# Convolution by single 128-channel blocks, a written order that reaches one group further, and another place for some tiles, in a two-layer decoder kernel

## The chip, the core and the metric

The kernel runs on one core of a Trainium2 chip. The metric is the device time of one execution in microseconds (us), as the median of three runs.

## What is computed

Two layers; in each, four parts add to the residual stream `h` (256 rows of 1024, float32):

```python
h = h + 0.5 * swiglu(rms_norm(h, ffn1_norm), w_gate_up, w_down)            # D_FF = 2816
u = rms_norm(h, mix_norm); q, k, v, ca, cg = split(u @ w_in)               # 512, 128, 128, 512, 512
attn = sliding_window_attention(rope(q), rope(k), v, sinks)                # 8 heads, 2 kv heads, window 128
conv = silu(layer_norm(depthwise_causal_conv31(ca * sigmoid(cg)) + b))     # 512 channels, 31 taps
h = h + concat(rms_norm(attn), rms_norm(conv)) @ w_out
h = h + 0.5 * swiglu(rms_norm(h, ffn2_norm), w_gate_up2, w_down2)
h = h + sigmoid(h @ w_gate) * rms_norm(p @ w_ple)
# after the layers: out = rms_norm(h, final_norm)
```

## The kernel before

The 256 rows are two blocks `t` of 128 rows. Nearly every product is made of three matmuls in the type fp32r: a float32 weight is split into a rounded part `hi` (a cast on ScalarE, ACT) and a rest `lo` (a subtraction on VectorE, DVE, or on GpSimd, POOL), the left operand likewise, and hi·hi, lo·hi and hi·lo are added in PSUM (`triple`, L262). Weights come by DMA in pieces of 512 KB into tiles tagged `raw` (4 buffers); `hi` and `lo` have 10 buffers each. A class `Unit` (L168) does this, either all at once (`load`, L174) or as named steps (`piece`, L208: `dma`, `hi`, `lo`, halves of 512 columns).

In every matmul of the projections and of the gate and up products the weights move through the array (512 columns, or 256) and a transposed block of the normalised input (`xh` or `xl`, 128 x 128) is stationary. In the down products the stationary tile is a slice of `hT_hi` or `hT_lo`, the transposed hidden block, and in the convolution's half of the output product it is a slice of `c_hi` or `c_lo`. These four come from the ring of tiles tagged `wr` (`wr`, L152; 4 buffers).

**The feed-forward stages** (`ffn_stage`, L425) run over 11 groups `j` of 256 hidden columns: load, gate and up for both row blocks (24 matmuls each), a transpose of the hidden block (`tr`, L449), the down products of the group before (24 matmuls). The compiler's scheduler orders all of this.

**The mixer stage** (`mixer_stage`, L652, `mixer`, L683) is different: the instructions of all five engines follow an order written out by hand, `PLAN` (L68), a list of step names. It begins inside the last two groups of the feed-forward stage before it (`dnb..`, `dnc..`, `fepi..`) and ends with the first group of the one behind it (`gu0`, `gu1`, with its loads `uf0`). Each engine does its own steps in that order. In it:

- the convolution's input comes in two column groups of 256 channels (`c0`, `c1`); `sig`, `u`, `ut`, `uT` gate and transpose it. Of the 31 taps the first 10 (8 in the second group) are done as a product on ACT (`pp`) that POOL adds up (`ya`), the rest as multiply-adds on DVE (`tap`, L756), each on two channel blocks of 128 in turn;
- `kv`, `q` with their rotary steps, then per head group the scores `s`, a fused mask-add and maximum on DVE (`ttr`, L875), `exp` on ACT, transposes `ptr`, copies `pT` (half on DVE, half on ACT), the products `pv`, the normalisation `o`;
- `ple`: float32 products for the layer's last part; `wa`, `wc`: the attention's and the convolution's half of the output product, then `xtr`, `xg`, `xh`, `xl` make the input of the next feed-forward stage.

`POOL_TAPS`, `QP`, `WCP` (L41 to L45) say which work POOL has: of `q` and `wc` it makes all `lo` halves. The softmax tiles `sm` (`sink`, L857) take two buffers of the `wr` ring for the first block and an own tag `pr` for the second. They are 2064 bytes per partition long, so the ring's buffers are 2080 bytes apart, the length rounded up to 32 bytes:

```python
            sm = wk.tile([P, n, NKV, P * (b + 1) + 1], F32, tag="wr" if b == 0 else "pr", name="sm",
                         bufs=NWR if b == 0 else 1)
```

The tiles' places follow from the order of the pools. In the built program the first weight tile stands at byte 44,960 of each partition, 32 beyond a multiple of 128; `xh` and `xl` also stand 32 beyond one, and the four `wr` buffers stand 32, 64, 96 and 0 beyond one.

Of the kernel before, what the change touches and what calls it, by code (L numbers as in the profile page):

```python
# [29 lines left out]
G = 4  # L30
# [10 lines left out]
POOL_TAPS = (10, 8)  # L41
C0P = ()
C1P = ()
QP = tuple(range(8))
WCP = tuple(range(4))  # L45
# [19 lines left out]
NPP = 2  # L65
# [27 lines left out]
rden1 pT100 yntr0 hwa01 ptr101 silu00 wa00.1 pT101 silu01 silu02 silu03 ptr111 hwa00 csq0 ptr110 pv100 ca0 pT111
chi0 fr0 pT110 clo0 yntr1 frs0 pv101 silu10 frr0 silu11 pv110 silu12 silu13 pv111 csq1 ca1 wc01.0 o1 chi1 clo1 osq1
wc01.1 rA1 fr1 hwc01 otr1 frs1 xtr01 frr1 oa1 wc00.0 xg01 wa11.0 wc00.1 uf0.hi3.0 uf0.hi3.1 wa11.1 uf0.lo3.0 hwc00
uf0.lo3.1 stat0 wa10.0 hwa11 uf0.hi2.0 rr0 uf0.hi2.1 wa10.1 uf0.lo2.0 uf0.lo2.1 xtr00 hwa10 wc11.0 xg00 xh00 wc11.1
xl00 wc10.0 xh01 hwc11 xl01 wc10.1 gu0.0 hwc10 stat1 xtr10 xtr11 xg10 gu0.1 rr1 xg11 xh10 xl10 gu0.2 xh11 gu0.3 xl11
gu1.0 sg0 h10 gu1.1 gu1.2 gu1.3 sg1 h11
# [4 lines left out]
def hybrid_trunk_kernel(  # L103
# [193 lines left out]

    ident = cp.tile([P, P], F32, name="ident")
# [126 lines left out]
    def ffn_stage(l, wgu, wdn, gname, side, early):  # L425
        X, r = [None, None], [None, None]
        H1, HT, DN, GU, acc = {}, {}, {}, {}, []
# [56 lines left out]
        def steps(does):  # L484

            GU[0] = unit_pair(wgu, 0, FF, KD)
            GU[0].steps("uf0", does)
            DN[0] = unit_plain(wdn, 0, 2, 0, D)
# [61 lines left out]

        def rest(nxt):
            for _ in range(2):
                acc.append([abank() for _ in range(2)])
            for j in range(NFC):
                if j > 0:
                    load(j)
                    gu(j, 0, GU[j])
                    tr(j - 1)
                if (j, 1) not in H1:
                    gu(j, 1, GU[j])  # L560
                if j in side:
# [64 lines left out]
    uT = [cp.tile([P, 2, CW - 1 + 256], F32, name=f"uT{e}") for e in range(2)]  # L626
# [3 lines left out]
    def mixer_consts():  # L630
# [8 lines left out]
        for e in range(2):  # L639
            GP.memset(uT[e][:, :, 0:CW - 1], 0.0)  # L640
# [11 lines left out]
    def mixer_stage(l, PT, EMB):  # L652
# [4 lines left out]
        c0 = unit_pair(w, 768, 1280, KD)  # L657
# [11 lines left out]
        def rest(nxt):  # L669
            c0.load(subs=2)  # L670
# [3 lines left out]
            mixer(l, w, X, r, r8, rotr, c0, PT, EMB, does)  # L674
# [8 lines left out]
    def mixer(l, w, X, r, r8, rotr, c0, PT, EMB, does):  # L683
# [3 lines left out]
        def halves(x, n=4):  # L687
# [19 lines left out]
        for name, label in (("c0", "c0t"), ("c1", "c1t"), ("kv", "kv"), ("q", "q")):  # L707
            for t in range(2):
                for s in range(KD // U[name].ku):
                    put(f"{label}{t}.{s}", part, name, t, s)  # L710

        def sig(e, t):
            tmp["sg", e, t] = wk.tile([P, FC], F32, tag="sg", name="sig", bufs=NSG)
            S.activation(tmp["sg", e, t], B[f"c{e}", t][:, FC:2 * FC], AF.Sigmoid, scale=r[t])

        def u(e, t):
            tmp["u", e, t] = wk.tile([P, FC], F32, tag="h1", name="u", bufs=NH1)
            V.scalar_tensor_tensor(out=tmp["u", e, t], in0=B[f"c{e}", t][:, 0:FC], scalar=r[t], in1=tmp["sg", e, t],
                                   op0=ALU.mult, op1=ALU.mult)

        def ut(e, t):
            if t == 0:
                tmp["ut", e] = tbank()
            for c in range(2):
# [3 lines left out]
        def to_uT(e):  # L728
            S.copy(uT[e][:, :, CW - 1:], halves(tmp["ut", e], 2))
# [508 lines left out]
```

## Time and profile before

| what | value |
|---|---|
| median of 3 runs | 1026.77 us (1026.62 to 1028.57) |
| the profiled execution's own time | 1029.06 us |
| its span, first to last instruction | 1027.2 us |
| TensorE (PE) busy | 998.3 us, 97% |
| DVE / ACT / POOL busy | 632.5 / 551.4 / 144.9 us |
| mean granted TensorE clock | 0.996 |

Times in the profile count from the first instruction. L12 is line 12 of the kernel. PE is the matmul, PEld the load of the stationary tile beside it. A matmul's recorded duration covers its way through a pipeline, so matmuls overlap; the pace is the distance of two starts. A matmul in plain float32 has two records, each of two passes.

### The profile page before, as it was taken

How to read it: one execution, taken by the hardware profiler on the slowest of the kernel's cores; microseconds unless marked ns; L12 is line 12 of the kernel's file. 1: busy time of each engine (PE TensorE's matmuls, PEld its weight loads, DVE VectorE, ACT ScalarE, POOL GpSimd, SP SyncE). 2: the span in 40 equal slices, each digit the busy share in tenths (PEclk: the TensorE clock that was granted, in tenths of full speed). 3: DMA queues.
4: the chain of work that ended last, by engine and by line, in shares of the span. 5: the costliest groups of instructions: out<-in, count | busy, mean ns of one | idle time of the engine just before them, and what ended most of it. 6: DMA issues, size and time to landing. Idle time of an engine off the chain costs nothing.

```text
span 1027.2 us, 13385 instructions
## 1 busy us (share of the span) xinstructions
PE 998.3 (97%) x4574; PEld 800.8 (78%) x4574; DVE 632.5 (62%) x1108; ACT 551.4 (54%) x1030; POOL 144.9 (14%) x195
## 2 busy tenths in 40 slices
PE   7999999999899999999999999999989999999996
PEld 5888888777577888888888888887857688888886
DVE  5864545679777554555775555547895955455553
ACT  6654444668754444445564445446885644444442
POOL 4300000067312000000000000001871300000001
PEclk9999999999999999999999999999999999999999
DMA  8865656444346565656556565644440666565621
GB/s 260 283 211 164 195 180 202 127 157 151 104 141 196 174 204 165 205 164 205 164 171 206 168 206 171 205 150 165 157 151 21 202 188 205 167 205 171 209 90 41
DMA packets 133172, 177.23 MB, mean 173 GB/s; under 512 B 8952, under 2 KB 109648, under 8 KB 133104
## 3 DMA queue, kind: packets, MB, share of 16 engines
q1 hardware_dynamic: 132016, 174.11, 53.1%
q0 software_dynamic: 1088, 2.27, 0.9%
q8 instruction: 36, 0.59, 0.2%
q14 instruction: 32, 0.26, 0.1%
HBM read 175.29 MB, written 1.05 MB: 172 GB/s over the span
## 4 chain that ended last, share of the span: by engine, by line
PE 89%; DVE 8%; DMA 1%; issue 1%; ACT 1%; SPq 0%; POOLq 0%; DVEq 0%; POOL 0%; ACTq 0%
PE bank L271 48%; PE abank L271 22%; PE bank L284 7%; PE bank L977 4%; DVE abank L756 3%; PE abank L525 2%; DVE lo L159 2%; PE tbank L453 2%; DMA raw<-in_ffn_w_gate_up_dram 1%; DVE xl L159 1%; DVE sm L875 1%; PE abank L907 1%; PE tbank L368 1%; PE tbank L396 0%; DVE xg L402 0%
## 5 line engine op out<-in xcount | busy, mean ns | idle before, releaser
L159 DVE TENSOR_TENSOR lo<-raw,hi 128x512 fp32r<-128x512 f32 (+1 forms) x507 | 378.5, 793 | 173.0 <-ACT hi L194 160.0
L194 ACT CAST hi<-raw 128x512 fp32r<-128x512 f32 (+1 forms) x464 | 303.4, 701 | 196.1 <-PE abank L271 118.2
L271 PE MATMUL bank<-hi,xh 128*128 128x512 f32 (+1 forms) x744 | 293.7, 395 | 1.4 <-ACT hi L194 1.2
L271 PE MATMUL bank<-hi,xl 128*128 128x512 f32 (+1 forms) x744 | 290.0, 390 | 1.0 <-DVE xl L159 1.0
L271 PE MATMUL bank<-lo,xh 128*128 128x512 f32 (+1 forms) x744 | 290.1, 390 | 0.3 <-POOL lo L159 0.2
L271 PEld LDWEIGHTS bank<-hi,xl 128*128 128x128 f32 x744 | 140.2, 188 | 31.0 <-DVE xl L159 2.2
L271 PEld LDWEIGHTS bank<-hi,xh 128*128 128x128 f32 x744 | 140.5, 189 | 29.7 <-ACT hi L194 1.6
L271 PEld LDWEIGHTS bank<-lo,xh 128*128 128x128 f32 x744 | 140.3, 189 | 29.5 <-POOL lo L159 1.3
L271 PE MATMUL abank<-hi,hT_hi 128*128 128x512 f32 x320 | 127.4, 398 | 0.0
L271 PE MATMUL abank<-lo,hT_hi 128*128 128x512 f32 x320 | 126.3, 395 | 0.0
L446 DVE SCALAR_TENSOR_TENSOR h<-bank,r,sg 128x256 f32<-128x256 f32 x84 | 40.5, 482 | 138.3 <-ACT sg L444 138.3
L271 PE MATMUL abank<-hi,hT_lo 128*128 128x512 f32 x320 | 125.5, 393 | 0.0
L444 ACT ACTIVATE sg<-bank,r 128x256 f32<-128x256 f32 x84 | 39.7, 473 | 159.5 <-PE bank L271 159.5
L348 POOL TENSOR_SCALAR ms_eps<-ms 128x1 f32<-128x1 f32 x24 | 6.6, 276 | 517.4 <-ACT scratch L355 208.4
L271 PEld LDWEIGHTS abank<-hi,hT_lo 128*128 128x128 f32 x320 | 60.2, 188 | 14.6
L271 PEld LDWEIGHTS abank<-hi,hT_hi 128*128 128x128 f32 x320 | 60.1, 188 | 13.6
L271 PEld LDWEIGHTS abank<-lo,hT_hi 128*128 128x128 f32 x320 | 60.2, 188 | 12.8
L756 DVE SCALAR_TENSOR_TENSOR abank<-uT,wconv,abank 128x256 f32<-128x256 f32 x168 | 69.2, 486 | 0.0
L284 PE MATMUL bank<-hi,xh 128*128 128x512 f32 (+1 forms) x160 | 62.0, 388 | 0.0
L284 PE MATMUL bank<-hi,xl 128*128 128x512 f32 (+1 forms) x160 | 59.3, 371 | 2.1 <-DVE xl L159 2.1
L284 PE MATMUL bank<-lo,xh 128*128 128x512 f32 (+1 forms) x160 | 59.0, 369 | 0.0
L227 ACT CAST hi<-raw 128x512 fp32r<-128x512 f32 x80 | 46.5, 615 | 21.2 <-PE bank L977 12.3
(183 smaller groups left out, 948.0 us busy)
## 6 DMA issues: line engine op xcount, KB each, us to landing
raw<-in_ffn_w_gate_up_dram SPq DMA_DIRECT2D x352, 256.0 KB, 4.0
raw<-in_ffn_w_down_dram SPq DMA_DIRECT2D x88, 512.0 KB, 5.4
raw<-in_w_in_dram SPq DMA_DIRECT2D x32, 256.0 KB, 3.8
raw<-in_w_out_dram SPq DMA_DIRECT2D x16, 512.0 KB, 4.9
raw<-in_w_ple_gate_dram SPq DMA_DIRECT2D x16, 512.0 KB, 4.2
raw<-in_w_in_dram SPq DMA_DIRECT2D x12, 512.0 KB, 4.6
raw<-in_w_ple_dram SPq DMA_DIRECT2D x4, 512.0 KB, 3.2
h<-in_x_dram SPq DMA_DIRECT2D x4, 256.0 KB, 4.5
```

The source lines that it names most:

```text
L159: return eng.tensor_tensor(out=lo, in0=src, in1=hi.bitcast(F32), op=ALU.subtract)
L194: S.copy(hi[:, sl, :], raw[:, sl, :])
L227: S.copy(half(sub[0], q), half(raw[0], q))
L271: T.matmul(dst, a, b, start=first and i == 0, stop=last and i == n - 1)
L284: T.matmul(dst, a, b, start=k == 0 and i == 0, stop=k == KD - 1 and i == 2)
L368: T.transpose(tb[:, i * P:(i + 1) * P], h[t][:, c * P:(c + 1) * P], ident)
L444: S.activation(s, b[:, 0:FC], AF.Silu, scale=r[t])
L446: V.scalar_tensor_tensor(out=o, in0=b[:, FC:2 * FC], scalar=r[t], in1=s, op0=ALU.mult, op1=ALU.mult)
L453: T.transpose(tb[:, k * 256 + t * P:k * 256 + (t + 1) * P], H1[j, t][:, k * P:(k + 1) * P], ident)
L525: T.matmul(acc[t][n], a, w_, start=False, stop=j == c and k == 1 and i == 2)
L756: V.scalar_tensor_tensor(out=acc, in0=src, scalar=ws, in1=acc, op0=ALU.mult, op1=ALU.add)
L977: T.matmul(B[name, t, n], a, b_, start=k == 0 and i == 0, stop=k == 3 and i == len(terms) - 1)
```

## The change

Four things change together.

1. **The convolution goes by blocks of 128 channels.** The group `c0` becomes `ca` and `cb` with 128 channels each (256 moving columns); `c1` becomes `cc`. `yp`, `pp`, `ya`, `tap` and `y` work on one block. 12, 12, 8 and 8 taps are POOL's, `pp` has 4 buffers.
2. **The order is new and longer**: 597 steps for 479. `kv` and `q` come before the third and fourth block. It takes in the loads `uf1` and the first 24 matmuls (`gux0`) of the second feed-forward group. The instructions of ACT and DVE that the groups `j` = 1 and 2 still trace are queued behind `sg1` and `h11` (`issue_after`: an order of issue on that engine, no wait).
3. **Work moves between engines**: the `lo` halves of `q` go from POOL to DVE, the copies `pT` all to ACT.
4. **Places**: the softmax tiles get tags of their own (`pr0`, `pr1`), their length rounded up to 128 bytes, so that the `wr` buffers are 2048 bytes apart; a tile of 96 bytes is put into the first pool, ahead of the weight and work pools. At the end `hf` and `o` take buffers of other tags.

```diff
-POOL_TAPS = (10, 8)
-QP = tuple(range(8))
+POOL_TAPS = (12, 12, 8, 8)
+QP = ()
+GROUPS = (("ca", (0,)), ("cb", (1,)), ("cc", (2, 3)))
-NPP = 2
+NPP = 4
...
+sigtab dnb11.0 ucb.dma0 ucb.dma1 ukv.dma0 ukv.dma1 dnb11.1 dnb00.0 ucb.hi0.0 dnb10.0 ucb.hi0.1 dnb10.1 ukv.hi0.0
...
+mxtr01 mxl00 uq.dma3 dnc10.1 mxg01 uq.hi1.0 mrr0 fepi10 uq.hi1.1 mxh01 fepi11 mxtr10 uq.hi2.0 mxl01 mxtr11 mrot0
+mxg10 uq.hi2.1 cat0.0 mxg11 mstat1 uq.lo0.1 cbt0.0 mxh10 uq.lo1.0 mrr1 ucc.dma0 uq.hi3.0 mxl10 uq.hi3.1 cbt0.1 mrot1
...
+uwc0.lo0.1 uwc1.hi0.0 uwc0.lo1.0 s00 uf0.dma0 sig20 ple00 ttr000 uwc1.hi0.1 u20 exptab uwc0.lo1.1 ttr001 ut20 ut21
+plesq00 uwc1.lo0.0 s01 uf0.dma1 s02 uT3 ttr010 uT2 ple10 tap3.8 yp3 uwc1.lo0.1 tap2.8 yp2 ttr011 tap2.9 pp3.1 ttr020
...
+pT111 tap2.30 pv101 uf0.lo1.0 silutab uf0.dma3 pv110 hwa00 uf0.lo1.1 pv111 y3 wa01.1 y2 uf1.dma0 o1 uf0.lo0.0 osq1
+otr1 uf0.lo0.1 rA1 ytr0 oa1 uf1.dma1 bn0 ytr1 wa10.0 bn1 lnr0 hwa01 lnr1 wa10.1 yn0 uf0.hi2.0 uf0.hi2.1 yn1 yntr0
...
+xl10 xtr11 gux0.0 xg11 gux0.1 xh11 xl11 gux0.2 gux0.3 gu0.2 sgx0 h1x0 gu1.0 gu0.3 gu1.1 sg0 h10 gu1.2 gu1.3 sg1 h11
...
+    cp.tile([P, 24], F32, name="pad")
     ident = cp.tile([P, P], F32, name="ident")
...
+        def one(j):
+            if j > 0 and (j, 0) not in H1:
+                load(j)
+                gu(j, 0, GU[j])
+            if j > 0:
+                tr(j - 1)
+            if (j, 1) not in H1:
+                gu(j, 1, GU[j])
...
             for j in range(NFC):
+                with ExitStack() as behind:
+                    for ins in last.values() if j == 1 or j == 2 else ():
+                        behind.enter_context(tc.issue_after(ins.ins))
+                    one(j)
...
-        c0 = unit_pair(w, 768, 1280, KD)
+        ca = unit_pair(w, 768, 1280, KD, cn=P)
...
-            c0.load(subs=2)
+            ca.load()
...
+        def pp(ch, k):
+            tmp["pp", ch, k] = wk.tile([P, 256], F32, tag="pp", name="pp", bufs=NPP)
+            S.activation(tmp["pp", ch, k], uT[ch][:, k:k + 256], AF.Copy, scale=wconv[l][:, ch:ch + 1, k])
+        def ya(ch, k):
+            GP.tensor_tensor(out=tmp["yp", ch], in0=tmp["yp", ch], in1=tmp["pp", ch, k], op=ALU.add)
...
         def sink(b, g0):
-            n = 2 if b == 0 else G
-            sm = wk.tile([P, n, NKV, P * (b + 1) + 1], F32, tag="wr" if b == 0 else "pr", name="sm",
-                         bufs=NWR if b == 0 else 1)
+            n, c = (2, P + 1) if b == 0 else (G, 2 * P + 1)
+            sm = wk.tile([P, -(-n * NKV * c // 32) * 32], F32, tag=f"pr{b}", name="sm", bufs=2 - b)
...
-            (V.tensor_copy if kv == 0 else S.copy)(tmp["pT", b, kc, kv], tmp["pt", b, kc, kv])
+            S.copy(tmp["pT", b, kc, kv], tmp["pt", b, kc, kv])
...
-                hf[t] = wk.tile([P, 512], F32, tag="pp", name="hf", bufs=NPP)
+                hf[t] = wf("hf")
-            o = wk.tile([P, 512], F32, tag="y", name="o", bufs=2)
+            o = wk.tile([P, 512], F32, tag="wr", name="o", bufs=NWR)
```

## Rows read from the trace of the kernel before

**Rows 1.** The page: busy time, share of the span, instructions.

```profile
PE 998.3 (97%) x4574; PEld 800.8 (78%) x4574; DVE 632.5 (62%) x1108; ACT 551.4 (54%) x1030; POOL 144.9 (14%) x195
```

**Rows 2.** Stretches of the span: length, each engine's busy time, clock, DMA.

```profile
22.50:190.40 167.90, 167.86 (x759) 137.66 (x760) 96.63 (x158) 82.82 (x139) 12.63 (x35) 1.00 0.64 200
...
190.40:316.40 126.00, 118.98 (x568) 88.97 (x567) 103.06 (x232) 88.92 (x204) 57.96 (x66) 1.00 0.42 138
...
692.40:820.00 127.60, 120.69 (x568) 89.77 (x567) 102.92 (x232) 88.77 (x203) 58.15 (x66) 0.99 0.42 137
...
204.90:243.00 38.10, 37.99 (x188) 30.83 (x187) 30.55 (x78) 27.75 (x65) 24.59 (x22) 1.00 0.47 165
243.00:268.20 25.20, 20.59 (x93) 13.08 (x92) 25.20 (x85) 20.51 (x57) 19.40 (x22) 1.00 0.45 148
...
770.00:785.00 15.00, 15.00 (x77) 10.09 (x75) 8.23 (x17) 10.19 (x29) 3.04 (x6) 0.89 0.11 35
```

**Rows 3.** The chain that ended last: start, length, engine, tile, line, count.

```profile
58.95 5.44 PE bank L271 x24
...
105.41 5.57 PE abank L271 x24
...
122.37 5.55 PE abank L271 x24
...
225.87 1.72 PE abank L271 x4
...
230.91 1.43 PE bank L284 x12
...
276.54 0.87 PE tbank L896 x8
277.42 0.84 PE abank L907 x8
...
282.33 2.84 PE bank L977 x12
```

**Rows 4.** The same chain, from 249 to 269 us.

```profile
249.49 0.26 DVE sm L875
...
257.54 0.40 DVE sm L875
...
260.32 0.79 DVE abank L756 x2
261.12 0.59 DVE pT L900
...
263.37 0.60 DVE lo L159
...
268.36 3.44 PE bank L977 x8
```

**Rows 5.** The same chain where the second mixer's output product begins.

```profile
770.62 4.89 PE bank L977 x8
```

**Rows 6.** What PE waited for: total us, times, longest.

```profile
PE bank L284 <- DVE xl L159: 2.1, 2, 1.1
...
PE tbank L396 <- DVE h L981: 0.8, 2, 0.4
```

**Rows 7.** Groups by line and form: busy us, mean ns, idle before.

```profile
L159 POOL TENSOR_TENSOR lo<-raw,hi 128x512 fp32r<-128x512 f32 x37 | 47.2, 1290 | 27.2 <-ACT hi L227 15.5 <-ACT hi L194 11.5
L227 ACT CAST hi<-raw 128x512 fp32r<-128x512 f32 x80 | 46.5, 615 | 21.2 <-PE bank L977 12.3 <-PE bank L271 3.1 <-DMA raw<-in_w_in_dram 1.8
L745 POOL TENSOR_TENSOR yp<-yp,pp 128x512 f32<-128x512 f32 x32 | 41.2, 1288 | 12.6 <-DVE abank L756 6.2 <-ACT pp L741 5.6
...
L741 ACT ACTIVATE pp<-uT,wconv 128x256 f32<-128x256 f32 x64 | 28.4, 502 | 2.4 <-POOL yp L745 2.1
...
L887 ACT ACTIVATE sm<-sm,nm 128x257 f32<-128x257 f32 x16 | 7.9, 497 | 0.1
...
L900 ACT COPY pT<-tbank 128x512 f32<-128x512 f32 x6 | 3.5, 579 | 1.7 <-PE tbank L896 1.7
```

More of the change, by code (lines that the diff above doesn't have):

```diff
@@ L94 @@
[L94 to L98, printed above, removed]
+sigtab dnb11.0 ucb.dma0 ucb.dma1 ukv.dma0 ukv.dma1 dnb11.1 dnb00.0 ucb.hi0.0 dnb10.0 ucb.hi0.1 dnb10.1 ukv.hi0.0
@@ new lines @@
+uf0.hi3.0 uf0.lo2.0 yntr1 silu00 hwa10 wa11.0 uf0.hi3.1 uf0.lo2.1 silu10 silu01 uf0.lo3.0 uf1.dma2 silu11 silu02
+wa11.1 uf0.lo3.1 silu12 silu03 silu13 ca0 csq0 uf1.dma3 ca1 csq1 fr0 hwa11 chi0 chi1 fr1 clo0 uf1.hi0.0 frs0 clo1
+wc00.0 uf1.hi2.0 frr0 uf1.hi0.1 frs1 uf1.hi2.1 uf1.lo0.0 wc00.1 frr1 uf1.lo2.0 wc01.0 hwc00 wc01.1 uf1.lo0.1
+uf1.lo2.1 xtr00 hwc01 wc10.0 xg00 stat0 xtr01 wc10.1 xh00 xg01 rr0 uf1.hi3.0 xl00 uf1.hi3.1 wc11.0 uf1.hi1.0
+uf1.lo3.0 xh01 hwc10 wc11.1 uf1.hi1.1 xl01 uf1.lo3.1 xtr10 hwc11 gu0.0 uf1.lo1.0 stat1 xg10 gu0.1 uf1.lo1.1 xh10 rr1
@@ L484, in steps @@
         def steps(does):
-            GU[0] = unit_pair(wgu, 0, FF, KD)
-            GU[0].steps("uf0", does)
-            DN[0] = unit_plain(wdn, 0, 2, 0, D)
+            for j in range(2):
+                GU[j] = unit_pair(wgu, j * FC, FF + j * FC, KD)
+                GU[j].steps(f"uf{j}", does)
+                DN[j] = unit_plain(wdn, 2 * j, 2, 0, D)
             tmp = {}
@@ L625, in hybrid_trunk_kernel @@
     v = [cp.tile([P, P], F32, name=f"v{t}") for t in range(2)]
-    uT = [cp.tile([P, 2, CW - 1 + 256], F32, name=f"uT{e}") for e in range(2)]
+    uT = [cp.tile([P, CW - 1 + 256], F32, name=f"uT{e}") for e in range(4)]
     wconv = [cp.tile([P, 4, CW], F32, name=f"wconv{l}") for l in range(DEPTH)]
@@ L638, in mixer_consts @@
                          base=128, channel_multiplier=1)
-        for e in range(2):
-            GP.memset(uT[e][:, :, 0:CW - 1], 0.0)
+        for e in range(4):
+            GP.memset(uT[e][:, 0:CW - 1], 0.0)
         GP.memset(kTz, 0.0)
@@ L673, in rest @@
                 does[f"mrot{t}"] = lambda t=t: rotary(t)
-            mixer(l, w, X, r, r8, rotr, c0, PT, EMB, does)
+            mixer(l, w, X, r, r8, rotr, ca, PT, EMB, does)
             nxt.steps(does)
@@ L681, in mixer_stage, with mixer @@
         return Stage(None, does, rest)
-    def mixer(l, w, X, r, r8, rotr, c0, PT, EMB, does):
+    def mixer(l, w, X, r, r8, rotr, ca, PT, EMB, does):
         def put(name, f, *args):
@@ L718, in u @@
[L718 removed]
+            name, chs = GROUPS[e]
+            n = len(chs) * P
+            tmp["u", e, t] = wk.tile([P, FC], F32, tag="h1", name="u", bufs=NH1)[:, 0:n]
+            V.scalar_tensor_tensor(out=tmp["u", e, t], in0=B[name, t][:, 0:n], scalar=r[t], in1=tmp["sg", e, t],
                                    op0=ALU.mult, op1=ALU.mult)
         def ut(e, t):
[L722 removed]
+            if ("ut", e) not in tmp:
@@ L758, in y, with to_uT, yp @@
-        def y(e):
-            Y[e] = wk.tile([P, 2, 256], F32, tag="y", name="y", bufs=2)
-            for c in range(2):
-                V.tensor_tensor(out=Y[e][:, c, :], in0=ACC[c][:, e * 256:(e + 1) * 256], in1=tmp["yp", e][:, c, :],
-                                op=ALU.add)
-        for e in range(2):
+        def to_uT(e, c):
+            S.copy(uT[GROUPS[e][1][c]][:, CW - 1:], tmp["ut", e][:, c * 256:(c + 1) * 256])
+        def yp(ch):
+            tmp["yp", ch] = wk.tile([P, 256], F32, tag="yp", name="yp", bufs=2)
+            S.activation(tmp["yp", ch], uT[ch][:, 0:256], AF.Identity, scale=wconv[l][:, ch:ch + 1, 0],
+                         bias=cb[:, ch:ch + 1])
@@ new lines, in pp, with tap @@
+        def pp(ch, k):
[3 more added lines that the diff above has]
+            GP.tensor_tensor(out=tmp["yp", ch], in0=tmp["yp", ch], in1=tmp["pp", ch, k], op=ALU.add)
+        def tap(ch, k):
+            if ch < 2 and k == POOL_TAPS[ch]:
+                ACC[ch] = abank()
+            acc, src = ACC[ch % 2][:, ch // 2 * 256:(ch // 2 + 1) * 256], uT[ch][:, k:k + 256]
+            ws = wconv[l][:, ch, k:k + 1]
+            if k == POOL_TAPS[ch]:
+                V.tensor_scalar(out=acc, in0=src, scalar1=ws, scalar2=None, op0=ALU.mult)
+            else:
+                V.scalar_tensor_tensor(out=acc, in0=src, scalar=ws, in1=acc, op0=ALU.mult, op1=ALU.add)
@@ L765, in mixer, with y @@
+        def y(ch):
+            Y[ch] = wk.tile([P, 256], F32, tag="y", name="y", bufs=4)
+            V.tensor_tensor(out=Y[ch], in0=ACC[ch % 2][:, ch // 2 * 256:(ch // 2 + 1) * 256], in1=tmp["yp", ch],
+                            op=ALU.add)
+        for e, (_, chs) in enumerate(GROUPS):
             for t in range(2):
```

182 lines of the change are left out of this document (79 added, 103 removed).

## The prediction, made before the result was known

> **What bounds the kernel now.** I read the page's busy times first: PE is busy 97% of the span [rows 1], so a change pays only where PE waits or where each of its matmuls is slow. Then the windows [rows 2]. In the feed-forward stage from 22.5 to 190.4 us PE lacks 0.04 us of 167.90; nothing that ACT, DVE or POOL do there can shorten it. The mixer in the hand-written order takes 126.0 us with PE busy 118.98, the second one 127.6 with 120.69: 7.0 and 6.9 us idle. Inside it PE loses 0.1 us up to 243.0, and 4.6 us (25.20 less 20.59) from there to 268.2, where DVE is busy 25.20 of 25.20; its chain there is taps, maxima, a copy and `lo` halves [rows 4]. The list of PE's waits names the end of the mixer: `gu0` waits for DVE's `xl` (2.1 us in 2 times) and the transposes for DVE's `h` (0.8 in 2) [rows 6].
>
> Last the pace. The chain shows groups of 24 matmuls of 512 columns with x stationary in 5.44 us, 226.7 ns each, and down products of the same shape in 5.57 and 5.55, so 231.6 [rows 3]. `wc` takes 2.84 for 12, 237. A 256-column matmul takes 1.43/12 = 119.2. A plain float32 record is 1.72/4 = 430 ns, two passes of 215. These differences between matmuls of one width have to come from their operands. The x tiles stand 32 bytes beyond a multiple of 128, the down products' stationary tiles 32, 64, 96 and 0.
>
> **Places (part 4).** 44,960 + 96 = 45,056 is a multiple of 128, so weights, x tiles and, at 2048 bytes apart, all `wr` tiles stand at 0. Stationary tiles of the down products then lie to their moving tiles as those of x do. I take it that this relation sets the pace: the 1056 down matmuls (4 stages x 11 groups x 24) go from 231.6 to 226.7, −5.2 us, and the 96 of `wc` (8 steps x 6 x 2 layers) gain perhaps 8 ns, −0.8. Sum −6.0. The bounds are wide: nothing, if place does not matter; 215 ns (the float32 pass) for every fp32r matmul of 512 columns, x ones too, which is −51 us; or the x matmuls take the down products' pace. All three are rivals below. The two kinds of group differ by 4.9 ns and the float32 pass by 11.7; the step of 4.9 is the one that two rows of the same kind of operand show, so I take it.
>
> **Where DVE bounds PE (parts 1 to 3).** I count the steps of the written order between the first `ple10` and `bn0`. Before: 22 tap operations at 0.395 = 8.7, 8 maxima at 0.26 and 8 at 0.40 = 5.3, two `lo` 1.2, a `pT` 0.59 [rows 4], and 3.5 for small ones (`o`, `oa`, `y`, `bn`, the query's rotation) priced as a `lo` or less: 19.3 us of DVE. PE has 12.1 there: two `ple` 3.4, and seven scores, transposes and value products at 0.43 to 0.87 [rows 3]. DVE is short by 7.2, of which 4.6 shows as idle PE [rows 2] since PE comes late to the stretch. After: 46 taps 18.2, 13 maxima 4.5, four `lo` 2.4, and 4.8 of small ones, 29.9 us; PE has 25.0, now three `ple` and four `wa` steps at 1.72, which is 12.0, and 13.0 of scores, transposes and value products. DVE is short by 4.9. But ACT fills too: from `ple00` to `silutab` it has 14 `pp` and 2 `yp`, which at 0.50 are 8.0, 16 `exp` at 0.50 or less 7.9, all six `pT` 3.5, seven casts at 0.615 4.3 [rows 7], and 13 others (two tables, squares) that I price as a `pp`, 6.5: 30.2 us at recorded durations, against 23.7 of PE, short by 6.5. I take 5.9, a little over the mean of the two, for 7.2 before: −1.3 per mixer, −2.6. Bounds: 4.9 for 7.2 is −4.6 in both mixers; 6.5 for the 4.6 that showed is +3.8.
>
> **The end of the mixer (part 2).** The waits for `xl` and `h`, 2.1 + 0.8 us, have only the 8 steps of `gu0` and `gu1` behind them, in the order's last lines. The new order puts 24 matmuls (`gux0`, 5.44 us) there, and casts and `lo` of the second group ahead. `gux0` needs the other row block only, so it runs while `xl10` and `xl11` are made: −2.9, bounds 0 and −2.9. What the covered work is late for next: the two `lo` halves of `uf1` stand ahead of `xg10` in DVE's queue, 1.2 us, covered by `wc11` (two steps of 1.4).
>
> **Costs.** (a) `ca` and `cb` have 256 columns: 96 matmuls at 119.2 instead of 48 at 226.7 are 11.44 for 10.88, +0.6 per mixer, +1.2. (b) The stretch from 204.9 to 243.0 has 38.0 of PE with DVE at 30.55 and POOL at 24.59 of 38.1 [rows 2]. DVE gets eight `lo` of `q` (4.8 us) and loses four tap operations and three copies (3.4) over the mixer; POOL loses eight `lo` of 1.29 and gains `ya` at half the width, 36 at between 0.64 (half of 1.288) and 1.288 for 16 at 1.288 [rows 7]: 23.0 to 46.4 for 20.6. If the half-width addition costs 0.75, POOL is lighter by 4. There is room on both, but the earlier order puts each `lo` closer to the matmul that reads it; I take +0.5 per mixer, +1.0, bounds 0 and +6 (the 15.5 us that POOL's `lo` waited for casts [rows 7] shows how late a cast can be; a fifth of it per mixer). (c) With more `wa` steps in it, the DVE-bound stretch is less sparse for PE. In the second mixer the granted clock falls to 0.89 between 770 and 785 [rows 2], and the same 8 float32 records take 4.89 us, 3.44 in the first [rows 4, 5]; 1.2 GHz was granted for part of it, after 25 us with a fifth of PE idle. I take half of that 1.45 back: −0.7, bounds 0 and −1.45.
>
> **Costed at nothing**, with the cover. The DMAs of `ca`/`cb` (two 512 KB pieces, in rows half as long) are issued under the 48 down matmuls of `dnb` and `dnc`, 11.1 us; if they land later, `cat0` waits and with it each step behind it on PE. `issue_after` queues the next groups' casts behind `sg1`, `h11`; 24 matmuls of `gu` and 24 of `gux0` are under way, 10.9 us; without that cover one cast and one `lo` are exposed, 1.2. The softmax's own tags free two `wr` buffers and add no wait. `hf` and `o` at the end wait for buffers idle by then.
>
> **Sum.** −6.0 −2.6 −2.9 +1.2 +1.0 −0.7 = −10.0. The profiled execution took 1029.06 (its span 1027.2 and 1.9 around it), 2.29 above the median; 1019.1 by it, and 1026.77 − 10.0 = **1016.8** for the median.
>
> **The rivals.** *The places move nothing.* The down products keep 5.55 to 5.57 and only the order counts: −4.0, 1022.8. For it: 5.57 and 5.55 take turns with the row block, whose tiles stand at different places, and the turn is worth only 1 ns a matmul. The Trainium skill, "SBUF — State Buffer", section "Specifications (TRN2)", gives lines of 16 bytes as the unit of access; a shift by 32 or 96 bytes is whole lines, so by that page this rival holds. The trace does not settle it: groups of one width differ by 4.9 ns.
>
> *Every fp32r matmul pays for standing 32 beyond 128.* Then the tiles at 0 go at the float32 pass's 215 ns: 2568 matmuls with x by 11.7 is 30.0, the 1056 down products by 16.6 is 17.5, some 3 for the rest, in all −51 and with the order −55: 972. Against it: float32 has another path, and one `wr` buffer stands at 0 already without a group at 5.2 us (24 x 215) in the chain; but its weights still stand at 32. Part of it is possible, any time between. The Trainium skill, "TensorE: Matmul & The Clock Gate", section "Back-to-back issue gap", gives columns / 2.4 GHz + 2.5 ns for an isolated gap; an estimate by that formula is 216 ns at 512, which is what the float32 row shows and 11 ns under the fp32r rows.
>
> *The new place is the bad one* (the other side). If 0 is worse for x than 32 is, the 2568 matmuls with x take the down products' pace: +12.6, and the −6.0 does not come; 1026.8 − 4.0 + 12.6 = 1035.4. It decides from 2.4 ns a matmul (6.1 us: −4.0 turns to +2). For it: the fastest groups of the trace all have their stationary tile at 32. Against: their moving tile stands at 32 as well, so the relation is kept.
>
> *The order loses*: ACT and DVE both full, 5 us on the wrong side at the bounds above, +3.8 +6 in place of −2.6 +1.0, is in the range, not a case of its own.
>
> **How the numbers follow.** The forecast has 0.45, with its own range 1010 to 1024; places that move nothing 0.25 (1017 to 1030); all or part of the float32 pace 0.15 (970 to 1010); the bad place 0.15 (1027 to 1038). A difference of 0.2%, 2 us, is about what a measurement of this kernel tells from none. Faster: 0.43 + 0.13 + 0.15 = 0.71; the same: 0.02 + 0.09 + 0.03 = 0.14; slower: 0.03 + 0.12 = 0.15. The range 985 to 1030 leaves out the full float32 pace (0.08) and most of the bad place (0.10).
>
> **What would show it.** In the chain the down groups of 24: 5.44 and the places are right, 5.55 and they move nothing, 5.2 with the gate and up groups at 5.2 too and it is the float32 pace, gate and up above 5.5 and the place is bad. `wc` in 2.72 for 2.84. In the windows, DVE and ACT full before `bn0`, with PE short of it by some 6 us; the waits for `xl` and `h` gone from PE's list; the clock 1.00 where the second mixer's output product begins. The prediction falls if the stretch before `bn0` loses over 8 us, if PE waits in the first third of the mixer for `lo`, or if the pace of the x groups moves at all.

## The result, and the profile after

The changed kernel takes 1018.86 us (median of 4 executions, 1017.86 to 1020.40), the kernel before 1026.69 (4, 1026.60 to 1028.57). The ratio is 0.9921 with a 95% interval of 0.9902 to 0.9939: 7.8 us faster, where 10.0 were forecast. The profiled execution took 1019.67 us for 1029.06, 9.4 less; the rows below are its own.

The page's busy times, with the same columns as [rows 1]:

```profile
PE 993.2 (98%) x4670; PEld 806.6 (79%) x4670; DVE 628.5 (62%) x1114; ACT 562.9 (55%) x1057; POOL 140.2 (14%) x221
```

The chain that ended last, columns as in [rows 3]:

```profile
104.21 5.44 PE abank L280 x24
109.65 5.44 PE bank L280 x24
...
211.47 1.44 PE bank L293 x12
...
245.37 1.72 PE abank L280 x4
...
278.81 3.45 PE bank L998 x8
```

The first row is a group of down products: 5.44 us, where [rows 3] have 5.57 and 5.55. The 256-column group takes 1.44 (1.43), and 4 float32 records 1.72 (1.72). The gate and up group right behind the down products takes 5.44 too. In the kernel before, such a group took 5.48 in the same place:

```profile
110.98 5.48 PE bank L271 x24
```

The starts of its matmuls show why: the first eight go at some 231 ns, the rest at 227. Of the 34 gate and up groups that stand right behind down products 17 had this slow start, and now one has. So the down products have changed pace, and the groups behind them have lost a trail of it, some 0.04 us each.

Windows, columns as in [rows 2]: the feed-forward stage, both mixers (with `gux0` now), then of the first mixer the stretch up to the first score, the one up to the output product, its middle, and three microseconds behind it:

```profile
21.78:188.50 166.72, 166.72 (x759) 137.53 (x760) 97.23 (x160) 89.11 (x147) 13.44 (x37) 1.00 0.64 202
188.50:319.60 131.10, 126.42 (x641) 97.34 (x640) 96.56 (x229) 85.52 (x206) 55.01 (x78) 0.99 0.38 124
688.10:817.40 129.30, 124.62 (x640) 96.14 (x639) 96.55 (x229) 85.51 (x205) 55.02 (x78) 1.00 0.39 126
202.80:244.80 42.00, 41.17 (x258) 36.84 (x257) 32.27 (x81) 30.60 (x67) 20.91 (x28) 1.00 0.53 176
244.80:278.60 33.80, 31.00 (x141) 18.95 (x140) 31.05 (x93) 29.82 (x86) 20.57 (x30) 1.00 0.27 81
250.00:270.00 20.00, 17.55 (x74) 9.82 (x73) 20.00 (x65) 20.00 (x67) 13.59 (x23) 1.00 0.09 27
290.00:293.00 3.00, 3.00 (x8) 2.32 (x8) 0.42 (x1) 0.36 (x1) 1.03 (x3) 0.51 0.00 0
```

From 250 to 270 us DVE and ACT are both busy 20.00 of 20.00. The last row has a granted clock of 0.51, so nearly all of it at 1.2 GHz, the lower of TensorE's two levels: 8 matmuls in 3 us. Just before, PE had run 16 single-column matmuls, with a wait of 0.2 us ahead of them. In [rows 2] such a stretch lay in the second mixer.

What PE waited for (us in all, times, longest):

```profile
PE bank L889 <- DVE m L896: 2.5, 4, 0.9
PE bank L293 <- DVE u L744: 1.6, 2, 0.8
...
PE tbank L1054 <- ACT sq L1049: 0.5, 2, 0.2
PE bank L280 <- DVE xl L168: 0.2, 1, 0.2
```

The waits for `xl` and `h` at the end of the mixer [rows 6] are gone but for 0.2 us; the one for `u` is new.

To set the kernels side by side I worked out from the starts of the matmuls what each stretch of a mixer loses: its length less its matmuls at pace (226.9 ns at 512 columns, 119.5 at 256, 430 for a float32 record of 512, 109 for a transpose). In us, first mixer / second mixer; a star marks a stretch with about 3 us at half clock:

| kernel | first column to first score | to the output product | to `gu0` | `gu0` to its end |
|---|---|---|---|---|
| before | 0.65 / 0.64 | 7.47 / 7.65 | 0.57 / 2.03* | 2.06 / 1.96 |
| changed | 1.43 / 1.37 | 5.97 / 5.97 | 2.19* / 0.54 | 0.26 / 0.22 |
| order alone (`a_order`) | 1.50 / 2.01 | 7.44* / 5.97 | 0.74 / 0.77 | 0.22 / 0.24 |
| places alone (`b_places`) | 0.69 / 0.65 | 7.46 / 7.76 | 0.37 / 1.78* | 2.07 / 2.05 |
| `a_nogux` | 1.40 / 1.40 | 5.98 / 5.98 | 0.53 / 0.55 | 0.18 / 0.18 |
| `a_noissue` | 1.41 / 1.41 | 5.97 / 5.97 | 0.54 / 0.54 | 0.22 / 0.22 |
| `a_pT` | 2.49 / 1.39 | 7.01 / 7.02 | 2.18* / 0.56 | 0.24 / 0.27 |
| `a_conv0` | 1.38 / 1.41 | 5.97 / 5.98 | 1.14 / 1.16 | 0.27 / 0.27 |
| `a_sigtab` | 0.35 / 0.39 | 5.97 / 5.98 | 0.54 / 2.14* | 0.22 / 0.27 |

### The profile page after: what moved, and what is told of

Read it like the earlier page. It is cut to its first block, busy times and chain, and to the rows that moved or that the text cites. A ratio compares the mean times of both kernels' runs of the same rounds, so it can differ in the third digit from the quotient of the medians.

```text
span 1017.9 us, 13621 instructions
## 1 busy us (share of the span) xinstructions
PE 993.2 (98%) x4670; PEld 806.6 (79%) x4670; DVE 628.5 (62%) x1114; ACT 562.9 (55%) x1057; POOL 140.2 (14%) x221
## 4 chain that ended last, share of the span: by engine, by line
PE 90%; DVE 5%; ACT 2%; DMA 1%; issue 1%; SPq 1%; POOL 0%; POOLq 0%; DVEq 0%; ACTq 0%
PE bank L280 47%; PE abank L280 22%; PE bank L293 11%; PE bank L998 4%; DVE abank L777 2%; PE tbank L463 2%; DMA raw<-in_ffn_w_gate_up_dram 1%; PE abank L540 1%; DVE sm L896 1%; PE abank L928 1%; DVE lo L168 1%; PE tbank L406 1%; PE tbank L378 1%; ACT co L1032 0%; PE tbank L1054 0%
## 5 line engine op out<-in xcount | busy, mean ns | idle before, releaser
L168 DVE TENSOR_TENSOR lo<-raw,hi 128x512 fp32r<-128x512 f32 (+1 forms) x523 | 385.6, 780 | 162.4 <-ACT hi L203 154.0
L203 ACT CAST hi<-raw 128x512 fp32r<-128x512 f32 (+1 forms) x448 | 293.8, 703 | 181.5 <-PE abank L280 101.7
L280 PE MATMUL bank<-hi,xh 128*128 128x512 f32 (+1 forms) x728 | 287.2, 394 | 1.7 <-ACT hi L203 1.1
L280 PE MATMUL bank<-hi,xl 128*128 128x512 f32 (+1 forms) x728 | 283.3, 389 | 0.2 <-DVE xl L168 0.2
L280 PE MATMUL bank<-lo,xh 128*128 128x512 f32 (+1 forms) x728 | 283.0, 389 | 0.1
L280 PEld LDWEIGHTS bank<-hi,xh 128*128 128x128 f32 x728 | 137.3, 189 | 29.5 <-ACT hi L203 2.0
L280 PEld LDWEIGHTS bank<-hi,xl 128*128 128x128 f32 x728 | 137.1, 188 | 29.2 <-DVE xl L168 1.0
L280 PEld LDWEIGHTS bank<-lo,xh 128*128 128x128 f32 x728 | 137.3, 189 | 27.2 <-DVE lo L168 0.6
L280 PE MATMUL abank<-hi,hT_hi 128*128 128x512 f32 x320 | 125.0, 391 | 0.0
L454 ACT ACTIVATE sg<-bank,r 128x256 f32<-128x256 f32 x82 | 38.9, 474 | 131.1 <-PE bank L280 131.1
L293 PE MATMUL bank<-hi,xh 128*128 128x512 f32 (+1 forms) x208 | 73.1, 351 | 1.6 <-DVE u L744 1.6
L293 PE MATMUL bank<-hi,xl 128*128 128x512 f32 (+1 forms) x208 | 70.9, 341 | 0.0
L293 PE MATMUL bank<-lo,xh 128*128 128x512 f32 (+1 forms) x208 | 70.8, 340 | 0.0
L236 ACT CAST hi<-raw 128x512 fp32r<-128x512 f32 x96 | 56.7, 624 | 17.6 <-PE bank L998 9.0
```

What stands on the lines that cost most here:

```text
L168: return eng.tensor_tensor(out=lo, in0=src, in1=hi.bitcast(F32), op=ALU.subtract)
L203: S.copy(hi[:, sl, :], raw[:, sl, :])
L236: S.copy(half(sub[0], q), half(raw[0], q))
L280: T.matmul(dst, a, b, start=first and i == 0, stop=last and i == n - 1)
L293: T.matmul(dst, a, b, start=k == 0 and i == 0, stop=k == KD - 1 and i == 2)
L454: S.activation(s, b[:, 0:FC], AF.Silu, scale=r[t])
```

## The experiments

Each ratio is to the kernel before, executed beside the run (medians 1027.04 to 1027.14).

### Places and order, each alone

`b_places` is the kernel before with both edits of place, `b_ring` with the softmax tiles' own tags alone, `b_pad` with the 96 bytes alone. `a_order` is the changed kernel without the 96 bytes and with the `wr` buffers 2080 bytes apart again; the softmax tiles keep their own tags in it.

```diff
 b_places, b_ring (before)
-            n = 2 if b == 0 else G
-            sm = wk.tile([P, n, NKV, P * (b + 1) + 1], F32, tag="wr" if b == 0 else "pr", name="sm",
-                         bufs=NWR if b == 0 else 1)
+            n, c = (2, P + 1) if b == 0 else (G, 2 * P + 1)
+            sm = wk.tile([P, -(-n * NKV * c // 32) * 32], F32, tag=f"pr{b}", name="sm", bufs=2 - b)
+            sm = sm[:, 0:n * NKV * c].rearrange("q (g a c) -> q g a c", g=n, a=NKV)
 b_places, b_pad (before)
+    cp.tile([P, 24], F32, name="pad")
 a_order (changed)
-    cp.tile([P, 24], F32, name="pad")
-        return wk.tile([P, 512], F32R, tag="wr", name=name, bufs=NWR)
+        return wk.tile([P, 520], F32R, tag="wr", name=name, bufs=NWR)[:, 0:512]
```

> The kernel before with the two edits of place alone (softmax tiles in tags of their own, so that the wr buffers stand 2048 bytes apart; the 96-byte tile). Theory: the places alone bring the down products' group of 24 from 5.56 to 5.44 us, 1056 matmuls by 4.9 ns, and the output product a little: 1026.7 - 5.2 - 0.8 = 1020.7 us, ratio 0.994. Rival, the new order is what sped them up (other neighbours, other tiles in flight): 5.56 stays, 1026.7. The mixer keeps its waits in both.

> The kernel before with the wr buffers 2048 bytes apart and no pad: every tile of the weight, x and wr pools stands 32 beyond a multiple of 128. Theory (what counts is where the stationary tiles stand to one another or to the weights): the down group of 24 takes 5.44 us as in the changed kernel, 1020.7 us. Rival (a multiple of 128 counts): 5.56 stays, 1026.7.

> The kernel before with the 96-byte tile alone: weights and x stand at a multiple of 128, the wr buffers 0, 32, 64 and 96 beyond one. Theory (relation): nothing changes, down groups 5.55 to 5.57, gate and up 5.44 to 5.49, 1026.7 us. Rival (a multiple of 128 counts): part of the 5.2 us of the down products comes with it, those in the buffer at 0 first, 1024 to 1026.

> The changed kernel without either edit of place (no 96-byte tile, wr buffers 2080 bytes apart again): order, engines and blocks alone. Theory: the down groups go back to 5.55 or more and the time to 1018.9 + 6.0 = 1024.9 us, so the order alone is worth about 2 us. Rival (places do nothing): 1018.9 stays.

Measured, as ratios to the kernel before: `b_places` 0.9951 (0.9936 to 0.9965), 1022.44 us; `b_ring` 0.9951 (0.9936 to 0.9966), 1022.01; `b_pad` 1.0003 (0.9993 to 1.0012), 1027.19; `a_order` 0.9990 (0.9981 to 0.9999), 1026.33. A group of down products in the chain of `b_places`, then of `b_ring`, `b_pad` and `a_order`:

```profile
103.99 5.44 PE abank L271 x24
```

```profile
104.59 5.44 PE abank L271 x24
```

```profile
104.72 5.57 PE abank L271 x24
...
121.69 5.55 PE abank L271 x24
```

```profile
105.18 5.57 PE abank L280 x24
```

The buffers 2048 bytes apart bring 5.44 with the old order, and without them the new order has 5.57. `b_ring` also frees the two `wr` buffers that the softmax tiles held; `a_order` has these free as well and keeps the slow pace, so it is the spacing that counts. The places are worth 0.49%, 5.0 us; the pad is worth nothing measurable.

The order alone is worth some 1 us, half of what was expected. On top of the places it is worth some 3 us (0.9921 for 0.9951), so the two do not simply add. Part of the difference shows in the profile of `a_order`: its two feed-forward stages between the mixers lose some 0.8 us more against pace than before. 8 of its 33 groups of down products go at 233.3 ns a matmul, where none did before, and 25 of the 34 gate and up groups behind them have the slow start, for 17. That `hT_hi` and `hT_lo` take other pairs of buffers there would explain it; it was not tried.

### Which distance counts

`a_shift` puts 64 bytes at the head of the work pool, `a_nopad` leaves out the 96, `a_xl` moves the first row block's `xl` by 64 inside a longer tile.

```diff
 a_shift
+    wk.tile([P, 16], F32, tag="gap", name="gap", bufs=1)
 a_nopad
-    cp.tile([P, 24], F32, name="pad")
 a_xl
-                    wk.tile([P, KD, P], F32R, tag=f"xl{t}", name=f"xl{t}", bufs=1))
+                    wk.tile([P, KD * P + 32], F32R, tag=f"xl{t}", name=f"xl{t}",
+                            bufs=1)[:, 16 * (1 - t):16 * (1 - t) + KD * P].rearrange("q (k m) -> q k m", k=KD))
```

> The changed kernel with 64 bytes put at the head of the work pool: weights stand at a multiple of 128, all stationary tiles (x and wr) 64 beyond one. Theory (the places of the stationary tiles hi and lo to one another set the pace): gate and up groups and down groups stay at 5.44 to 5.49 us, 1018.9 us. Rival (their place relative to the moving weights counts): all 3500 matmuls change pace, by 4.9 ns each +17 us, or towards the float32 pass of 215 ns, -40 us.

> The changed kernel without the 96-byte tile: all tiles 32 beyond a multiple of 128, wr buffers 2048 bytes apart. Theory (relation): no change, 1018.9 us, down groups 5.44. Rival (the multiple of 128 adds something in the new order, a cast, a tap or a transfer that crosses a line): +1 us or more.

> The changed kernel with xl of the first row block alone 64 bytes on (xh, the second block, weights and wr tiles stay at a multiple of 128). One matmul in three of that block has a stationary tile at another place than the weights. Theory A (each such matmul costs 6.3 ns, as all did with every stationary tile 64 on): the block's group of 24 goes from 5.44 to 5.49, +2.6 us in all, 1021.5. Theory B (a triple with its two stationary tiles at two places loses as the down products did, 13 to 15 ns): 5.55, +6 us, 1024.9. The second block's groups stay at 5.44 to 5.49 in both.

Measured: `a_shift` 1.0118 (1.0104 to 1.0132), 1039.35 us; `a_nopad` 0.9937 (0.9923 to 0.9950), 1021.01; `a_xl` 1.0018 (1.0009 to 1.0027), 1029.48. Chain of `a_shift`, then of `a_xl`:

```profile
106.27 5.60 PE abank L280 x24
111.87 5.60 PE bank L280 x24
...
215.77 1.42 PE bank L293 x12
```

```profile
94.19 5.54 PE bank L280 x24
100.17 5.57 PE bank L280 x24
105.74 5.44 PE abank L280 x24
...
117.15 5.59 PE bank L280 x24
122.74 5.48 PE abank L280 x24
```

`a_shift` refutes the theory as it was put and bears out its rival: the hi and lo tiles still stand alike, yet each matmul of 512 columns takes 233.3 ns instead of 227. Some 3600 of them make 23 us, of which 20.5 were measured. The 256-column group loses nothing (1.42 for 1.44), and the first matmuls behind a transposition were slower than 227 ns without the shift too. What counts is the distance between stationary tile and moving weights.

In `a_xl` the first block's groups take 5.54 (5.44 in the changed kernel), nearer to theory B's 5.55 than to A's 5.49. But the second block's groups, meant as the control, take 5.57 to 5.59. The longer tile had moved them by 128 bytes, and the `wr` tiles by 256, as the order and the lengths of the tiles give it; the trace holds no addresses. Taken by the distance to the weights modulo 512 bytes, all kernels fall into one list at 512 columns: 0 gives 226.9 ns a matmul, 128 gives 232.6, 64 gives 233.3, and `xh` at 0 with `xl` at 64 gives 230.9 on average. The `wr` buffers before stood at distances 0, 32, 64 and 96 (231.8).

256 is as good as 0. The down products of `a_xl`, at that distance, take 5.44 and 5.48 in turn, 228 ns on average, but in a group of 5.48 only the first eight matmuls are slow, behind a gate and up group of the slow pace; the rest go at 227, as in a group of 5.44. So a multiple of 128, as the prediction had it, is not enough and one of 256 was; 2080 to 2048 was right since 2048 is such a multiple. Other distances were not tried, and why the distance matters is open.

`a_nopad` has the pace of the changed kernel, and its losses in the mixers are within 0.3 us of the changed kernel's (1.40 / 1.69, 5.97 / 5.98, 2.16* / 0.53, 0.21 / 0.21). Its interval overlaps with the changed kernel's; whether the pad is worth a microsecond or two in the new order stays open.

### What cleared the end of the mixer

```diff
 a_nogux: PLAN without gux0.0 to gux0.3, sgx0, h1x0; the scheduler places that work
 a_noissue
-                    for ins in last.values() if j == 1 or j == 2 else ():
+                    for ins in last.values() if False else ():
```

> The changed kernel with the 24 matmuls of gux0 and their sgx0, h1x0 taken out of the written order; the scheduler places them behind. Theory (they cover the making of the second row block's x at the end of the mixer): the loss in the last stretch of each mixer goes from 0.2 back to some 1.8 us, 1018.9 + 3.2 = 1022.1 us. Rival (the earlier work had thinned out already and the end is free without them): 1018.9.

> The changed kernel without the order of issue behind sg1 and h11: casts and subtractions of the groups 1 and 2 may go ahead on ACT and DVE again. Theory (it is this that keeps DVE free for xl at the end of the mixer, since the kernel without gux0 showed no such wait either): the loss from gu0 on goes from 0.2 back towards 2.0 us per mixer, 1018.9 + up to 3.6 = 1022.5 us. Rival (the written order, which makes x earlier, is enough): 0.2 and 1018.9 stay.

Both theories fell. `a_nogux`: 0.9918 (0.9903 to 0.9933), 1018.61 us, loss at the end 0.18. `a_noissue`: 0.9921 (0.9906 to 0.9935), 1019.33, loss 0.22. Neither part is needed. DVE's timeline of the kernel before (start, length, what) shows what stood there:

```profile
301.16 2.50 DVE L159 TENSOR_TENSOR lo<-raw,hi 128x512 fp32r<-128x512 f32 x4
303.56 0.75 DVE L981 SCALAR_TENSOR_TENSOR h<-bank,r,h 128x512 f32<-128x512 f32 x1
304.23 2.35 DVE L159 TENSOR_TENSOR lo<-raw,hi 128x1024 fp32r<-128x1024 f32 x2
306.49 1.29 DVE L402 TENSOR_TENSOR xg<-tbank,pcol 128x512 f32<-128x512 f32 x2
307.87 3.83 DVE L159 TENSOR_TENSOR xl<-xg,xh 128x512 fp32r<-128x512 f32 x2
```

Six subtractions of the next group, 4.85 us, stand ahead of the second block's `xg`. In the changed kernel the same stretch of DVE reads:

```profile
302.38 0.75 DVE L1002 SCALAR_TENSOR_TENSOR h<-bank,r,h 128x512 f32<-128x512 f32 x1 [0.26 <-PE bank L998]
303.04 0.68 DVE L168 TENSOR_TENSOR lo<-raw,hi 128x512 fp32r<-128x512 f32 x1
303.64 0.68 DVE L412 TENSOR_TENSOR xg<-tbank,pcol 128x512 f32<-128x512 f32 x1
304.24 0.68 DVE L168 TENSOR_TENSOR lo<-raw,hi 128x512 fp32r<-128x512 f32 x1
305.01 0.69 DVE L168 TENSOR_TENSOR xl<-xg,xh 128x512 fp32r<-128x512 f32 x1
```

One at a time, between the steps of x. That the written places of `uf1`'s steps among `xg`, `xh` and `xl` make the difference is read from these rows; it was not tried alone, nor were `gux0` and the order of issue taken out together.

### Who bounds the stretch before the output product

```diff
 a_pT
-            S.copy(tmp["pT", b, kc, kv], tmp["pt", b, kc, kv])
+            (V.tensor_copy if kv == 0 else S.copy)(tmp["pT", b, kc, kv], tmp["pt", b, kc, kv])
```

> The changed kernel with three of the six copies pT of each mixer on DVE again, as before. Between the first score and the last transpose ahead of the output product, PE loses 5.97 us per mixer; ACT and DVE are both busy 20 of 20 us from 250 to 270. Theory (DVE is short there): DVE gets 1.8 us more and PE loses up to that, 7.5 us, 1018.9 + 3 = 1022. Rival (ACT is short): PE loses 4.5 to 5.9, 1016 to 1018.9.

0.9932 (0.9917 to 0.9947), 1021.11 us, 2.3 above the changed kernel. The loss rises from 5.97 to 7.01 in both mixers. Busy times in its middle (columns as above):

```profile
251.00:271.00 20.00, 17.11 (x70) 9.39 (x69) 20.00 (x63) 19.30 (x65) 14.15 (x24) 1.00 0.09 28
```

ACT, full before, has 0.7 us free now, DVE none: DVE is short, and the copies belong on ACT. With two engines at 20.00 of 20.00 the busy columns could not say this. In the first mixer 1.1 us more are lost ahead of the scores too, for a reason that I did not find.

### Two edits that the profile suggested

```diff
 a_conv0
-silu00 hwa10 wa11.0 ... silu10 silu01 ... silu11 silu02 wa11.1 ... silu12 silu03 silu13 ca0 csq0 uf1.dma3 ca1 csq1
-fr0 hwa11 chi0 chi1 fr1 clo0 uf1.hi0.0 frs0 clo1 wc00.0 uf1.hi2.0 frr0 ... wc00.1
+silu00 hwa10 wa11.0 ... silu01 ... silu02 silu03 wa11.1 ... ca0 chi0 csq0 silu10 clo0 silu11 hwa11 wc00.0 silu12
+silu13 fr0 frs0 frr0 ca1 chi1 csq1 uf1.dma3 clo1 wc00.1 uf1.hi0.0 uf1.hi2.0 fr1 frs1 ...
 a_sigtab
-sigtab dnb11.0 ucb.dma0 ...
+dnb11.0 ucb.dma0 ... sink0b sigtab ucb.lo1.0 ...
```

> The changed kernel with another order of the convolution's last steps: the four silu of the first row block, its ca, chi, csq and clo ahead of those of the second, the first half of wc00 ahead of fr0, and fr1 behind wc00. PE lost 0.83 us there waiting for the square on ACT, then ran 16 single-column matmuls in a row, behind which the first mixer's granted clock was 0.51 from 290 to 293 us. Theory: the wait goes (-0.5 to -0.8 per mixer) and the low clock comes less often: 1016 to 1018 us. Rival (ACT is the bound there, PE only waits elsewhere): 1018.9.

> The changed kernel with the step that loads ACT's sigmoid table moved from the head of the order to behind sink0b, in the last down products of the stage before. In the changed kernel that load ran at 46 us, in the middle of the first feed-forward stage, was replaced by the next silu's table, and the table came again at 207.5 us, 1.28 us in which the first sigmoid, DVE's product behind it and PE's kv0.0 waited (0.8 us of PE, twice). Theory: the 0.8 us of each mixer goes: 1018.9 - 1.6 = 1017.3 us; the loss between the first column and the first score falls from 1.4 to about 0.6. Rival (kv0.0 waits for DVE's queue anyway): 1018.9 and 1.4.

`a_conv0`: 0.9929 (0.9916 to 0.9941), 1019.87 us. There is no half-clock stretch in its profile, and none of its five executions has a mean granted clock under 0.997, where two of the changed kernel's four have 0.996. But the loss ahead of `gu0` is 1.15 in each mixer where the changed kernel has 0.54 without such a stretch, and PE waits longer for the square. The line of PE's waits, then ACT's timeline:

```profile
PE tbank L1054 <- ACT sq L1049: 1.1, 2, 0.5
```

```profile
290.03 0.62 ACT L1041 CAST c_hi<-a 128x512 fp32r<-128x512 f32 x1 [1.67 <-DVE a L1037]
290.55 0.63 ACT L1049 ACTIVATE sq<-co 128x512 f32<-128x512 f32 x1
```

On the time the expectation failed. In the new order the square stands behind the cast `c_hi` in ACT's queue, and that cast waits 1.67 us for DVE's `a`. So the second row block's square ends at 291.18, and PE waits 0.5 us for it. On the clock five executions are too few to say.

`a_sigtab` started from ACT's timeline of the changed kernel:

```profile
46.12 1.28 ACT L350 ACT_TABLE_LOAD   x1
47.64 1.28 ACT L640 ACT_TABLE_LOAD   x1
49.52 1.28 ACT L454 ACT_TABLE_LOAD   x1
...
207.48 1.28 ACT L738 ACT_TABLE_LOAD   x1 [0.53 <-PE bank L293]
208.78 0.37 ACT L738 ACTIVATE sig<-bank,r 128x128 f32<-128x128 f32 x1
```

The step `sigtab` at the head of the order depends on nothing and had run at 46 us. The sine of the rotary tables (L640) and then the next silu (L454) took the table away, and the first sigmoid fetched it again, with PE waiting. Moved, the load lies here:

```profile
194.81 1.28 ACT L350 ACT_TABLE_LOAD   x1
```

0.9911 (0.9897 to 0.9925), 1017.79 us. The loss up to the first score falls from 1.4 to 0.35 and 0.39, more than the 0.6 expected, and the wait for `u` is gone from PE's list. It is the fastest kernel here by its median; its interval overlaps with the changed kernel's, so the gain of some 2 us is shown by the two profiles' stretches and not by the times. All five of its executions have a mean clock of 0.996 or less, for two of four of the changed kernel: the half-clock stretches may take part of the gain back.

## Why the prediction came out as it did

The time lies 2.1 us above the forecast and in its own range. By its steps, against the profiled execution (−9.4):

| step | forecast | profile |
|---|---|---|
| down products | −5.2 | 1056 x (231.8 − 227.0) = −5.1 |
| groups behind the down products | not named | −0.6 (17 slow starts before, one now) |
| `wc` | −0.8 | 96 x (233.2 − 228.7) = −0.4 |
| wait for the square ahead of `wc` | not named | about +0.4 |
| stretch before the output product | −2.6 | −1.5 −1.7 = −3.2 |
| end of the mixer | −2.9 | −1.8 −1.7 = −3.5 |
| 256-column groups | +1.2 | +1.2 |
| earlier stretch | +1.0 | +0.8 +0.7 = +1.5 |
| clock | −0.7 | +0.2: the stretch moved to the first mixer |

The rows of the profile make −9.5. `b_places` shows the gain of `wc` by itself (0.57 to 0.37 per mixer); in the changed kernel the same stretch takes 0.54, since PE now waits there for the square, which the prediction did not price. The 8 ns a matmul for `wc` were twice too many: they came from 237 ns, 2.84 us for 12, which holds a gap, and by the starts of the matmuls the gain was 4.5 ns. That the sum came so near is luck in part: three terms that each brought 0.6 more than was forecast (the stretch, the end, the groups behind the down products) stand against `wc`, the square and the earlier stretch, which together brought 1.3 less.

**Places.** The step held, in pace and size, with the relation of stationary and moving tile as its cause, which `a_shift` and `b_ring` show. That it came out at 2048 bytes is in part luck: the unit of 128 that the prediction worked with would have been wrong for tiles 128 apart (`a_xl`). The pace of the gate and up groups behind the down products moved a little with it (5.48 to 5.44), which the prediction had counted as a sign against itself; it is the trail of the same cause. The rival that places move nothing is out: against the changed kernel 64 bytes cost 2% (1.0118 for 0.9921). For it stood the Trainium skill, "SBUF — State Buffer", section "Specifications (TRN2)", with cachelines of 16 bytes, by which a shift of whole lines should be harmless; the trace differs (233.3 for 226.9 ns). The rivals by the place itself are out too: with all tiles at 32 (`b_ring`) the pace is that at 0 (`b_places`), and no fp32r group came near the float32 pass.

**The stretch.** Right in sign and nearly in size. DVE's count gave 4.9 us of shortfall and ACT's 6.5; 5.97 was lost. `a_pT` shows that DVE is the shorter of the two, so its count came out some 1 us low. ACT's, at recorded durations, came out too high: with work taken off ACT the loss did not fall.

**The end.** The size was near (−2.9 for −3.5), the cause was not: I put it down to `gux0`, and without `gux0` the waits stay gone. DVE's rows show six subtractions of the next group that no longer stand ahead of `xg`; that this alone clears the end was not tried.

**The earlier stretch.** Again the size was near and the cause wrong. I had priced `lo` halves that come late; the loss is one table load of 1.28 us per mixer in front of the first sigmoid, which costs PE 1.0 us (`a_sigtab`). `sigtab` stands as the first word of the new order in the diff, and the prediction has no term for it: I had not asked from when on nothing holds it back. The Trainium skill, "ScalarE: Activation LUTs", section "What ACT_TABLE_LOAD costs", gives about 1283 ns for the load and about 1380 ns for a drain with it. The trace agrees on 1.28 and shows no drain behind the load: the sigmoid starts 0.02 us after it.

**The clock.** Half of 1.45 us was expected back, and none came. Of the fourteen profiles of this case nine have one such stretch while PE works and none has two. It lies in either mixer, in the tap stretch or in the output product, and costs 1.4 to 1.7 us in the table of losses. No edit was shown to remove it. It comes in some executions of a kernel and not in others: of the 43 executions of the kernel before that stand beside the runs, 36 have a mean clock of 0.997 to 0.999 and took 1026.8 to 1027.6 us, and seven have 0.996 and took 1028.7 to 1029.1.

**7.8 for 9.4.** Both profiled executions have a half-clock stretch, so the 9.4 compare like with like. The medians do not: by the 43 executions above, 1026.69 is a time without the stretch, while the changed kernel's median lies between two executions at a clock of 0.996 (1019.67 and 1020.40) and two at 0.997 and 0.998 (1018.05 and 1017.86). Without the stretch on either side, 1026.60 and 1017.86 are 8.7 apart. With the clock left aside the forecast was 9.3 (10.0 less 0.7), and 8.7 to 9.4 came, by few executions: the miss of the median is the clock for the most part.

## What to carry to other kernels

In a tile pool, look at the distance between a matmul's stationary and moving tiles: a stray 32 bytes in the length of the buffers cost every down product 2%, and giving the odd-sized tiles a tag of their own gave it back without touching the order. When two engines are full at once, take a little work from one to the other: the loss tells which of them is short. In an order written by hand a step without inputs has no earliest time, so put a table load behind something that holds it.

## What was not expected of the hardware

The pace of fp32r matmuls of 512 columns depends on the distance of their two operands: 226.9 ns at 0 and, once under way, at 256 bytes, 232.6 at 128, 233.3 at 64. At 256 columns no loss showed (1.42 us for 12 at a distance of 64, 1.44 at 0). A disturbed stream takes about eight matmuls, at some 231 ns, to come back to 227. About 3 us at half clock came once in nine of fourteen profiled executions, at no fixed place in the two mixers: 0.51 from 290 to 293 us here, 0.50 from 785 to 787 in `a_sigtab`. It parts the executions of the kernel before into two groups of times, 1026.8 to 1027.6 and 1028.7 to 1029.1.
